# A fixed TensorE order around three places of a hybrid attention block

## The chip, the cores and the metric

The kernel runs on one core of a Trainium2 chip as one program. The metric is device time in microseconds (us) from launch to the end of the program, and smaller is better. The kernel before took 788.79 us (median of three runs, 788.05 to 789.27). Engines are written as in the profile: PE is TensorE's matmuls, PEld its weight loads, DVE is VectorE, ACT is ScalarE, POOL is GpSimd, and SP is the engine whose queue issues most of the transfers.

## The reference, cut to what matters

One block works on 512 tokens of width 1024 in float32. The normed input is projected to the inputs of two mixers. The first is a gated linear attention (GLA) with 4 heads, run forward and backward in chunks. The second is a latent attention (MLA) with 8 heads, whose queries and keys come from normed latents `cq` and `ckv`. Both are gated and added, projected by `w_out` and added to the input. Then follow a norm, an MLP and a last norm:

```python
y_gla = gla_branch(gq, gk, gv, gr, z_gf, z_gb, ...)
y_mla = mla_branch(cq, ckv, kr, positions, ...)
merged = jax.nn.sigmoid(z_ma) * y_gla + jax.nn.sigmoid(z_mb) * y_mla
h = h + merged @ w_out[l]
m = rmsnorm(h, g_mlp[l])
h = h + jnp.square(jax.nn.relu(m @ w_ff1[l])) @ w_ff2[l]
return rmsnorm(h, g_final)
```

In `mla_branch` the query latent is normed before its projection: `q = (rmsnorm(cq, g_q) @ w_uq)`. In `gla_direction` the decayed queries and keys of a chunk give `scores`, which are masked and then multiplied by `v`.

## The kernel before

Every large product is done as three matmuls in the fp32r form (`mm3`, L90): each factor is split into a high half, which ACT writes (`split`, L95, and `split_scaled`, L99: lines L96 and L100), and a rest, which DVE writes (L97, L101). Transposes, GLA scores and feature sums are plain f32 matmuls, which PE runs in two passes. Tokens lie in four row tiles of 128, `h0` to `h3` in the profile's `h`.

Tiles come from pools with a fixed number of buffers. The PSUM pool has two tags, `mm` and `at`, of four banks each. A new tile of a tag takes the bank of the fourth tile before it, so its first matmul waits until that tile has been read for the last time. Weight halves (`wh`, `wl`) have four buffers each, and raw weights (`wf`) three.

The program is written in Python and ordered by a scheduler, which estimates when instructions can start and writes one fixed sequence per engine. On the chip each engine takes its own sequence strictly in that order. An instruction that waits for a semaphore holds everything behind it on its engine. `in_program_order` (L103) can pin a stretch of the program to the order in which it is written, on all engines.

Four places matter here.

**GLA scores** (`gla_scores`, L460). For head h, `bd` gets the four backward diagonal blocks (L463). ACT copies it to `bds`. Then each of four row tiles `sc` gets three matmuls (L475, L476, L477). The second and third read `qk` tiles that POOL scales last (L432). DVE writes the masked backward part into `sc` (`copy_predicated`, L481), and ACT and DVE split `sc` into halves for the output product `gla_out` (L538, tiles `gla..o`). In the main loop the scores of a head come before the gate projection `zb` of feature `2h` (`mla_g2`), which is followed by the gates of the next head (`gatef`, `gateb`, L379) and `zb` of feature `2h+1`. For head 2 the values `gv` are projected just before the scores.

**Query latent** (head 3, `latent`, L568). The sums of squares of `cq` (tile `cqss`) go through DVE and POOL to a diagonal matrix `cqdg` (L257). Two matmuls with ones spread it to `cqrs` (L266). DVE scales the latent (`cqc`, L586), it is split into `cqhl`, and the rotary projections `ro` read it.

**MLP transposes** (`rows_product`, L831, `normed`, L871, and `Flipped`). The second column half of `w_out` ends row by row (tiles `wo`, banks of tag `at`): when a row tile is complete, DVE adds it to `h` (L859), ACT sums squares (L156), DVE and POOL make the row factor (`hp`, L163 and L166), and DVE writes the normed row `ms` (L876). PE then transposes the row in eight pieces into `mb` (L181), and after two rows ACT and DVE split `mb` into the `mT` halves (L100, L101). The first two hidden tiles of the MLP, `f00` and `f01`, run on token halves, so that they can start when rows 0 and 1 are there. DMA loads of the next weights (`f02f` and so on, and 16 pieces `w` of `w_ff2`) stand in SP's queue between.

**The last group.** The second MLP product runs in seven Strassen-like products per group. `prep` makes the halves of the weights for the product after next. In the last group `last_rows` (L1018) pins its order: the last rows are added, squared and scaled (`out_square`, `out_store`), row 1 in two column halves `ge` and `gend`, and the output goes out in eight transfers.

Of the kernel before, what the change touches and what calls it, by code (L numbers as in the profile page):

```python
# [15 lines left out]
ALU = mybir.AluOpType  # L16
AX = mybir.AxisListType

P = 128
S = 512  # L20
NT = S // P
D = 1024
KD = D // P
# [36 lines left out]
def tile_block(ctx: ExitStack, tc: tile.TileContext, t, out: bass.AP):  # L60
    nc = tc.nc
# [38 lines left out]
        nc.scalar.activation(hi, src, AF.Copy, scale=scale)  # L100
        nc.vector.scalar_tensor_tensor(lo, src, scale, raw(hi), op0=ALU.mult, op1=ALU.subtract)  # L101

    def in_program_order(start):  # L103

        prev = {}
        for ins in nc.cur_bb.bb.instructions[start:]:
            before = prev.get(ins.engine)
            if before is not None:
                tc.add_manual_dep(
                    ins, before,  # L110
                    mybir.DependencyInfo(mybir.DependencyClass.NoSync, mybir.DependencyReason.DATA),
                    reason="program order",
                )
            prev[ins.engine] = ins.name


    ident = one([P, P], F32, "ident")
# [96 lines left out]
        wh, wl = weights(w[:, col : col + P], name)  # L214
        return wh, wl, ps(tag, name)

    def proj_run(begun, src, half=None):
        wh, wl, acc = begun
        c = slice(0, S) if half is None else slice(half * 256, half * 256 + 256)
        for k in range(KD):  # L220
            mm3(acc[:, c], wh[:, k, :], wl[:, k, :], src[k][:, 0, c], src[k][:, 1, c], k == 0, k == KD - 1)
        return acc

# [61 lines left out]
    def v_evict(acc, hl, i):  # L285
        split_scaled(hl[:, 0, :], hl[:, 1, :], acc, r_x[:, i : i + 1])

    fixed = len(nc.cur_bb.bb.instructions)
    warm = ps("at", "warm")
    for _ in range(8):  # L290
        nc.tensor.matmul(warm[:, :P], ident, ident, start=True, stop=True)
# [20 lines left out]
    for k in range(KD):  # L312
        wh, wl = (vh[k // 2][x][:, k % 2, :] for x in range(2))
# [220 lines left out]
    def mla_g2(f):  # L534

        return gated(proj_T(C_ZB + f * P, f"zb{f}"), f"b{f}")[1]
# [124 lines left out]
    merged = [None] * MH  # L661
# [98 lines left out]
    y1, g2 = [], []  # L760
# [5 lines left out]
    for h in range(GH):  # L766
        last = h == GH - 1
        if h:
            g1 = gla_g1(h, (0,))
            waiting = gla_rstd(*waiting)  # L770
            g1 += gla_g1(h, (1,))
            y1 += gla_norm(*waiting)
        if h == GH - 2:
            cos, sin = rotary_tables()
        near, nxt, far = gla_qk(h, parts)
        if last:
            ckv_steps, cq_steps = latent(C_CKV, 2, V_KV, "ckv"), latent(C_CQ, 3, V_Q, "cq")
            next(ckv_steps)
            next(ckv_steps)
            next(cq_steps)  # L780
            ckv = next(ckv_steps)
            next(cq_steps)
        if h == 2:
            v = gla_v(1)
        if last:
            cq = next(cq_steps)
        sc = gla_scores(near, nxt, far)
        g2.append(mla_g2(2 * h))
        if last:
            kbuf = rotary_k()  # L790
            ro = rotary_q()
        else:
            parts = gate_parts(h + 1)
        g2.append(mla_g2(2 * h + 1))
        if last:
            for _ in up_units(0):
                pass
        waiting = gla_out(h, sc, v, g1, f"gla{h}"), g1, f"gla{h}"
# [24 lines left out]
    hrow = []  # L823
# [4 lines left out]

    hparts = {}

    def rows_product(lhs, w, nk, name, first_done, done):  # L831
        for c in range(2):
            accs = [ps(("mm", "at")[c], f"{name}{c}{i}") for i in range(NT)]

            def piece(i, k2, wh, wl):
                tok = slice(i * P, (i + 1) * P)
                for kk in range(2):
                    k = 2 * k2 + kk
                    mm3(accs[i], lhs[k][:, 0, tok], lhs[k][:, 1, tok], wh[:, kk, :], wl[:, kk, :],
                        k == 0, k == nk - 1)  # L840

            staggered = 2 if c == 1 else 0
            kept = []
            for k2 in range(nk // 2):
                wh, wl = weights(w[k2 * 2 * P : (k2 + 1) * 2 * P, c * S : (c + 1) * S], f"{name}{c}{k2}")
                if k2 >= nk // 2 - staggered:
                    kept.append((k2, wh, wl))
                    continue
                for i in range(NT):
                    piece(i, k2, wh, wl)  # L850
            for i in range(NT):
                for k2, wh, wl in kept:
                    piece(i, k2, wh, wl)
                add_rows(i, c, accs[i])
                (first_done, done)[c](i)

    def add_rows(i, c, acc):
        hc = hrow[i][:, c * S : (c + 1) * S]
# [12 lines left out]
    def normed(i):  # L871
        m = ms_rows[i]
        square_half(hrow[i], 1, hparts[i], m)
        rs = row_rstd(hparts[i])
        for c in range(2):
            nc.vector.tensor_scalar(  # L876
                m[:, c * S : (c + 1) * S], hrow[i][:, c * S : (c + 1) * S], rs, None, op0=ALU.mult
            )
        fm.rows(i, m)
        if i % 2 == 1:  # L880
            fm.evacuate(i // 2)

    rows_product(merged, t["w_out"][0], KD, "wo", first_half_square, normed)

# [130 lines left out]

    def last_rows(left, right4, right2, x_accs):  # L1018

        begun = len(nc.cur_bb.bb.instructions)  # L1020
        for rb in range(2):
            block_product(4, left, right4, x_accs, False, rb)
            add_rows(2 + rb, 0, x_accs[rb])
            out_square(2 + rb, slice(0, S))
        e_accs = [ps("mm", f"ge{rb}") for rb in range(2)]
        parts = e_accs[1], ps("at", "gend")
        block_product(2, left, right2, e_accs, True, 0)
        out_store(2)
        add_rows(0, 0, e_accs[0])
        out_square(0, slice(0, S))  # L1030
        out_store(3)
        for x in range(2):
            cols = slice(x * HT, (x + 1) * HT)
            block_product(2, left, right2, [None, parts[x]], True, 1, cols, slice(0, HT))
            nc.vector.tensor_tensor(hrow[1][:, cols], parts[x][:, 0:HT], hrow[1][:, cols], op=ALU.add)
            out_square(1, cols, x == 1)
            out_store(x)
        in_program_order(begun)

    early = [proj_begin(w1, j * P, f"f0{j}", "at") for j in range(2)]  # L1040
    for half in range(2):
        for begun in early:
            proj_run(begun, mT, half)
    for x in (B11, B12, B22, B21):
        load_w2(0, x)
    for qd in range(NQ):
# [12 lines left out]
        xs_ = [ps("at", f"gx{qd}{rb}") for rb in range(2)]  # L1059
        zs_ = [ps("at", f"gz{qd}{rb}") for rb in range(2)]  # L1060
        for n, m in enumerate(ORDER):
            if n + 2 < len(ORDER):
                right[ORDER[n + 2]] = prep(ORDER[n + 2], qd)
            if m == 2:
                accs, begin = [ps("mm", f"gw{qd}{rb}") for rb in range(2)], True
            elif m == 4 and last:
# [4 lines left out]
            for rb in range(2):  # L1071
                block_product(m, left, right[m], accs, begin, rb)
                upper, lower = rb, 2 + rb
                if m in (1, 2):
                    add_rows(upper, 0, accs[rb])
                elif m in (6, 3):
                    add_rows(upper, 1, accs[rb])
                elif m in (5, 7):
                    add_rows(lower, 1, accs[rb])
                if m == 4:  # L1080
                    add_rows(lower, 0, accs[rb])
                if last and m in (3, 7):
                    out_first(upper if m == 3 else lower)


def build(arrays):
# [21 lines left out]
```

## Time and profile before

| | |
|---|---|
| Median of three runs | 788.79 us (788.05 to 789.27) |
| Profiled execution: its time | 788.01 us |
| Profiled execution: its span, first to last instruction | 786.3 us |
| PE busy | 773.6 us (98%) |
| PE weight loads busy | 647.6 us (82%) |
| DVE busy | 546.4 us (69%) |
| ACT busy | 409.4 us (52%) |
| POOL busy | 104.4 us (13%) |
| Granted TensorE clock, mean | 0.998 |

The profiled execution took 0.78 us less than the median, and 1.7 us of it lie outside the span. Rows of a timeline read: start in us from the span's start, duration in us, engine, source line, operation, output<-inputs, shapes, count, and in brackets the idle time of the engine just before and what ended it. Neighbouring matmuls overlap in these rows, so their spacing is read from their starts. Line numbers are those of the kernel before.

### The profile page before, as it was taken

Reading aid. Unit: us, or ns where it says so; the run is one execution under the profiler, and the core shown is the slowest. Engines: PE = TensorE matmul, PEld = TensorE weight load, DVE = VectorE, ACT = ScalarE, POOL = GpSimd, SP = SyncE. Lnnn points to the kernel's source line nnn. Section 1 sums busy time; section 2 is a strip of 40 time slices with the busy share of each in tenths; the row PEclk is TensorE's granted clock in tenths of the full one; section 3 lists DMA queues with packets and bytes.
Section 4 is the critical chain, followed back from the end, with each engine's and each line's share of the span. In section 5 each row is a group of like instructions: output and inputs, shape, how many; then the busy total and the mean of one; then the engine's idle time right before and its main releaser. Section 6 shows DMA issues by size and latency. Waiting matters only on the chain.

```text
span 786.3 us, 10004 instructions
## 1 busy us (share of the span) xinstructions
PE 773.6 (98%) x3736; PEld 647.6 (82%) x3736; DVE 546.4 (69%) x839; ACT 409.4 (52%) x685; POOL 104.4 (13%) x168
## 2 busy tenths in 40 slices
PE   9999999999999999999999999999999999999995
PEld 7888888888888878888888888888888888888884
DVE  7767657575565449799973677875787578848785
ACT  8463624523562326698853466535554465336644
POOL 1023203213031214211120100000000000000023
PEclk9999999999999999999999999999999999999999
DMA  7633232233223422513032731164106510560002
GB/s 256 169 85 81 55 90 72 79 94 108 73 62 81 74 46 52 131 55 108 28 135 85 267 105 54 54 185 136 51 15 202 142 48 27 173 176 0 28 1 107
DMA packets 102385, 74.47 MB, mean 95 GB/s; under 512 B 14976, under 2 KB 86656, under 8 KB 102336
## 3 DMA queue, kind: packets, MB, share of 16 engines
q1 hardware_dynamic: 101248, 70.66, 31.5%
q10 hardware_dynamic: 864, 2.38, 0.8%
q0 software_dynamic: 224, 0.79, 0.3%
q8 instruction: 29, 0.48, 0.2%
q14 instruction: 20, 0.16, 0.1%
HBM read 69.62 MB, written 2.10 MB: 91 GB/s over the span
## 4 chain that ended last, share of the span: by engine, by line
PE 92%; issue 3%; DVE 2%; POOL 1%; ACT 1%; POOLq 0%; DVEq 0%
PE f L92 7%; PE f L93 7%; PE f L91 7%; PE gx L91 4%; PE gx L93 4%; PE gx L92 4%; PE gv L301 3%; PE gr L91 2%; PE gr L93 2%; PE gr L92 2%; PE za L93 2%; PE gz L93 2%; PE gz L92 2%; PE gz L91 2%; PE za L92 2%
## 5 line engine op out<-in xcount | busy, mean ns | idle before, releaser
L904 DVE TENSOR_TENSOR w<-w,w 128x1024 f32<-128x1024 f32 x32 | 38.8, 1222 | 0.4
L1058 POOL DMA_DIRECT2D gfin<-in_g_final x1 | 0.7, 653 | 282.7 <-PE f L93 282.7
L725 ACT ACTIVATE e<-s,top 128x512 f32<-128x512 f32 x32 | 21.9, 685 | 6.0 <-DVE top L722 5.1
L97 DVE TENSOR_TENSOR pT<-tp,pT 128x512 fp32r<-128x512 f32 x32 | 21.7, 680 | 0.5 <-ACT pT L96 0.4
L859 DVE TENSOR_TENSOR h<-gx,h 128x512 f32<-128x512 f32 x32 | 21.6, 685 | 0.5 <-PE gx L93 0.4
L722 DVE TENSOR_REDUCE top<-s 128x1 f32<-128x512 f32 x32 | 21.7, 680 | 0.1
L96 ACT ACTIVATE pT<-tp 128x512 fp32r<-128x512 f32 x32 | 18.9, 592 | 3.1 <-PE tp L739 2.9
L739 PE MATMUL tp<-ident,e 128*128 128x128 f32 x128 | 19.2, 273 | 0.1
L91 PE MATMUL av<-pT,v 128*128 128x256 f32 x64 | 19.3, 301 | 0.0
L757 POOL TENSOR_TENSOR tb<-tb,g 128x512 f32<-128x512 f32 x8 | 11.1, 1382 | 56.9 <-DVE tb L756 43.8
L739 PEld LDWEIGHTS tp<-ident,e 128*128 128x128 f32 x128 | 15.3, 140 | 3.9 <-DVE pT L97 0.5
L952 ACT ACTIVATE fa<-f 128x512 f32<-128x512 f32 x32 | 18.5, 577 | 0.0
L92 PE MATMUL av<-pT,v 128*128 128x256 f32 x64 | 18.4, 288 | 0.0
L516 DVE TENSOR_TENSOR za<-za,R 128x512 f32<-128x512 f32 x8 | 5.5, 691 | 18.4 <-PE za L93 18.4
L93 PE MATMUL av<-pT,v 128*128 128x256 f32 x64 | 18.1, 283 | 0.0
L96 ACT ACTIVATE gbh<-y 128x512 fp32r<-128x512 f32 x16 | 10.1, 633 | 14.0 <-DVE y L969 14.0
L432 POOL TENSOR_TENSOR qk<-qkf,e3f 128x256 f32<-128x256 f32 x8 | 7.8, 972 | 63.8 <-DVE qkf L424 63.8
L96 ACT ACTIVATE sc<-sc 128x512 fp32r<-128x512 f32 x16 | 8.8, 599 | 10.6 <-DVE sc L481 10.6
L96 ACT ACTIVATE b_00h<-w 128x1024 fp32r<-128x1024 f32 x7 | 7.4, 1060 | 12.9 <-PE gz L93 6.0
L91 PE MATMUL s<-kbuf,q 128*128 128x512 f32 x32 | 13.7, 428 | 0.3 <-DVE pT L97 0.3
L961 ACT ACTIVATE px<-fa 128x256 f32<-128x256 f32 x32 | 13.4, 419 | 1.0
L96 ACT ACTIVATE b_10h<-w 128x1024 fp32r<-128x1024 f32 x7 | 7.4, 1060 | 12.1 <-PE gz L93 6.0
(1460 smaller groups left out, 2805.6 us busy)
## 6 DMA issues: line engine op xcount, KB each, us to landing
w<-in_w_ff SPq DMA_DIRECT2D x64, 256.0 KB, 3.6
x<-in_xt SPq DMA_DIRECT2D x8, 256.0 KB, 5.2
vw<-in_w_in SPq DMA_DIRECT2D x8, 256.0 KB, 5.3
q<-ro SPq DMA_DIRECT2D x16, 128.0 KB, 4.9
h<-in_x ACTq DMA_DIRECT2D x4, 512.0 KB, 4.7
out<-ms SPq DMA_DIRECT2D x7, 256.0 KB, 2.3
gr0f<-in_w_in SPq DMA_DIRECT2D x1, 512.0 KB, 4.8
za0f<-in_w_in SPq DMA_DIRECT2D x1, 512.0 KB, 5.7
```

The costliest lines, as they stand in the source:

```text
L91: nc.tensor.matmul(acc, lh, rh, start=start, stop=False, skip_group_check=onto)
L92: nc.tensor.matmul(acc, lh, rl, start=False, stop=False, skip_group_check=onto)
L93: nc.tensor.matmul(acc, ll, rh, start=False, stop=stop, skip_group_check=onto)
L96: nc.scalar.activation(hi, src, AF.Copy)
L97: rest.tensor_tensor(lo, src, raw(hi), op=ALU.subtract)
L301: nc.tensor.matmul(v_accs[i], a[:, i * P : (i + 1) * P], b, start=k == 0 and x == 0, stop=k == KD - 1 and x == 2)
L722: nc.vector.tensor_reduce(top, acc, axis=AX.X, op=ALU.max, negate=True)
L725: nc.scalar.activation(e, acc, AF.Exp, bias=top, accum_out=tot)
L739: nc.tensor.transpose(tp[:, k * P : (k + 1) * P], e[:, k * P : (k + 1) * P], ident)
L859: nc.vector.tensor_tensor(hc, acc, hc, op=ALU.add)
L904: nc.vector.tensor_tensor(wq[dst][g], wq[x][g], wq[y][g], op=op)
L952: nc.scalar.activation(a, acc, AF.Relu)
```

## The change

Four edits; no arithmetic is added or taken away.

1. For heads 0, 1 and 3 the gate projection `zb` of feature `2h` is written ahead of the scores, and a helper `tensor_engine_goes_on` makes PE's first scores matmul come after the last matmul of that projection. Head 2 keeps its order.
2. For head 3 the spreading of the query latent's factor is written behind the scores, and PE is made to take it after them.
3. In `rows_product` the last two k-steps of the second column half are regrouped. Rows 0 and 1 are completed first. Row 2 runs its first half, then come the transposes of row 0, then its second half; row 3 likewise around the transposes of row 1. The transposes of rows 2 and 3 move behind five of the eight k-steps of `f01` on the first token half. `f00` and `f01` alternate by k on the second half. PE is pinned to this order from the start of the regrouped part to the end of `f01`; the other engines are left to the scheduler.
4. In the last group, `prep` for product 2 is written behind the additions of product 7 (before, ahead of the product). In `last_rows`, row 1's two column halves are now added one behind the other, then squared one behind the other, and then rows 0 and 1 are stored.

```diff
--- before.py
+++ after.py
@@ -100,18 +100,34 @@
         nc.scalar.activation(hi, src, AF.Copy, scale=scale)
         nc.vector.scalar_tensor_tensor(lo, src, scale, raw(hi), op0=ALU.mult, op1=ALU.subtract)
 
-    def in_program_order(start):
+    def issued_after(ins, before):
+        tc.add_manual_dep(
+            ins, before,
+            mybir.DependencyInfo(mybir.DependencyClass.NoSync, mybir.DependencyReason.DATA),
+            reason="program order",
+        )
+
+    def traced():
+        return len(nc.cur_bb.bb.instructions)
+
+    def in_program_order(start, engines=None):
 
         prev = {}
         for ins in nc.cur_bb.bb.instructions[start:]:
+            if engines is not None and ins.engine not in engines:
+                continue
             before = prev.get(ins.engine)
             if before is not None:
-                tc.add_manual_dep(
-                    ins, before,
-                    mybir.DependencyInfo(mybir.DependencyClass.NoSync, mybir.DependencyReason.DATA),
-                    reason="program order",
-                )
+                issued_after(ins, before)
             prev[ins.engine] = ins.name
+
+    PE_ONLY = (mybir.EngineType.PE,)
+
+    def tensor_engine_goes_on(start, mid):
+
+        ins = nc.cur_bb.bb.instructions
+        pe = [[i for i in part if i.engine in PE_ONLY] for part in (ins[start:mid], ins[mid:])]
+        issued_after(pe[1][0], pe[0][-1].name)
 
 
     ident = one([P, P], F32, "ident")
@@ -214,10 +230,10 @@
         wh, wl = weights(w[:, col : col + P], name)
         return wh, wl, ps(tag, name)
 
-    def proj_run(begun, src, half=None):
+    def proj_run(begun, src, half=None, ks=range(KD)):
         wh, wl, acc = begun
         c = slice(0, S) if half is None else slice(half * 256, half * 256 + 256)
-        for k in range(KD):
+        for k in ks:
             mm3(acc[:, c], wh[:, k, :], wl[:, k, :], src[k][:, 0, c], src[k][:, 1, c], k == 0, k == KD - 1)
         return acc
 
@@ -285,7 +301,7 @@
     def v_evict(acc, hl, i):
         split_scaled(hl[:, 0, :], hl[:, 1, :], acc, r_x[:, i : i + 1])
 
-    fixed = len(nc.cur_bb.bb.instructions)
+    fixed = traced()
     warm = ps("at", "warm")
     for _ in range(8):
         nc.tensor.matmul(warm[:, :P], ident, ident, start=True, stop=True)
@@ -782,11 +798,19 @@
             next(cq_steps)
         if h == 2:
             v = gla_v(1)
+        begun = traced()
+        if h == 2:
+            sc = gla_scores(near, nxt, far)
+            g2.append(mla_g2(2 * h))
+        else:
+            g2.append(mla_g2(2 * h))
+            gated_at = traced()
+            sc = gla_scores(near, nxt, far)
+            tensor_engine_goes_on(begun, gated_at)
         if last:
+            scored_at = traced()
             cq = next(cq_steps)
-        sc = gla_scores(near, nxt, far)
-        g2.append(mla_g2(2 * h))
-        if last:
+            tensor_engine_goes_on(gated_at, scored_at)
             kbuf = rotary_k()
             ro = rotary_q()
         else:
@@ -828,7 +852,7 @@
 
     hparts = {}
 
-    def rows_product(lhs, w, nk, name, first_done, done):
+    def rows_product(lhs, w, nk, name, first_done, done, flip):
         for c in range(2):
             accs = [ps(("mm", "at")[c], f"{name}{c}{i}") for i in range(NT)]
 
@@ -848,11 +872,33 @@
                     continue
                 for i in range(NT):
                     piece(i, k2, wh, wl)
-            for i in range(NT):
-                for k2, wh, wl in kept:
-                    piece(i, k2, wh, wl)
+            if c == 0:
+                for i in range(NT):
+                    add_rows(i, c, accs[i])
+                    first_done(i)
+                continue
+            begun = traced()
+            ks = [(2 * k2 + kk, wh[:, kk, :], wl[:, kk, :]) for k2, wh, wl in kept for kk in range(2)]
+
+            def part(i, which):
+                tok = slice(i * P, (i + 1) * P)
+                for k, wh, wl in ks[which]:
+                    mm3(accs[i], lhs[k][:, 0, tok], lhs[k][:, 1, tok], wh, wl, k == 0, k == nk - 1)
+
+            def complete(i):
                 add_rows(i, c, accs[i])
-                (first_done, done)[c](i)
+                done(i)
+
+            whole, first, rest = slice(0, 4), slice(0, 2), slice(2, 4)
+            for i in range(2):
+                part(i, whole)
+                complete(i)
+            for i in range(2):
+                part(2 + i, first)
+                flip(i)
+                part(2 + i, rest)
+                complete(2 + i)
+            return begun
 
     def add_rows(i, c, acc):
         hc = hrow[i][:, c * S : (c + 1) * S]
@@ -876,11 +922,13 @@
             nc.vector.tensor_scalar(
                 m[:, c * S : (c + 1) * S], hrow[i][:, c * S : (c + 1) * S], rs, None, op0=ALU.mult
             )
-        fm.rows(i, m)
+
+    def flipped(i):
+        fm.rows(i, ms_rows[i])
         if i % 2 == 1:
             fm.evacuate(i // 2)
 
-    rows_product(merged, t["w_out"][0], KD, "wo", first_half_square, normed)
+    begun = rows_product(merged, t["w_out"][0], KD, "wo", first_half_square, normed, flipped)
 
 
 
@@ -1017,7 +1065,7 @@
 
     def last_rows(left, right4, right2, x_accs):
 
-        begun = len(nc.cur_bb.bb.instructions)
+        begun = traced()
         for rb in range(2):
             block_product(4, left, right4, x_accs, False, rb)
             add_rows(2 + rb, 0, x_accs[rb])
@@ -1029,18 +1077,26 @@
         add_rows(0, 0, e_accs[0])
         out_square(0, slice(0, S))
         out_store(3)
+        cols = [slice(x * HT, (x + 1) * HT) for x in range(2)]
         for x in range(2):
-            cols = slice(x * HT, (x + 1) * HT)
-            block_product(2, left, right2, [None, parts[x]], True, 1, cols, slice(0, HT))
-            nc.vector.tensor_tensor(hrow[1][:, cols], parts[x][:, 0:HT], hrow[1][:, cols], op=ALU.add)
-            out_square(1, cols, x == 1)
+            block_product(2, left, right2, [None, parts[x]], True, 1, cols[x], slice(0, HT))
+            nc.vector.tensor_tensor(hrow[1][:, cols[x]], parts[x][:, 0:HT], hrow[1][:, cols[x]], op=ALU.add)
+        for x in range(2):
+            out_square(1, cols[x], x == 1)
+        for x in range(2):
             out_store(x)
         in_program_order(begun)
 
     early = [proj_begin(w1, j * P, f"f0{j}", "at") for j in range(2)]
-    for half in range(2):
-        for begun in early:
-            proj_run(begun, mT, half)
+    proj_run(early[0], mT, 0)
+    proj_run(early[1], mT, 0, range(5))
+    flipped(2)
+    flipped(3)
+    proj_run(early[1], mT, 0, range(5, KD))
+    for k in range(KD):
+        for e in early:
+            proj_run(e, mT, 1, (k,))
+    in_program_order(begun, PE_ONLY)
     for x in (B11, B12, B22, B21):
         load_w2(0, x)
     for qd in range(NQ):
@@ -1059,8 +1115,10 @@
         xs_ = [ps("at", f"gx{qd}{rb}") for rb in range(2)]
         zs_ = [ps("at", f"gz{qd}{rb}") for rb in range(2)]
         for n, m in enumerate(ORDER):
-            if n + 2 < len(ORDER):
-                right[ORDER[n + 2]] = prep(ORDER[n + 2], qd)
+            ahead = ORDER[n + 2] if n + 2 < len(ORDER) else None
+            behind = last and ahead == 2
+            if ahead and not behind:
+                right[ahead] = prep(ahead, qd)
             if m == 2:
                 accs, begin = [ps("mm", f"gw{qd}{rb}") for rb in range(2)], True
             elif m == 4 and last:
@@ -1081,6 +1139,8 @@
                     add_rows(lower, 0, accs[rb])
                 if last and m in (3, 7):
                     out_first(upper if m == 3 else lower)
+            if behind:
+                right[ahead] = prep(ahead, qd)
 
 
 def build(arrays):
```

## The prediction

> **What bounds the kernel now.** I read the page first: the span and the chain that ended last.
>
> ```profile
> span 786.3 us, 10004 instructions
> PE 92%; issue 3%; DVE 2%; POOL 1%; ACT 1%; POOLq 0%; DVEq 0%
> ```
>
> PE is the bound nearly everywhere, and no edit takes a matmul away. So the change can win only where PE stands still, or behind its last matmul. The waits of PE come next; columns are the sum in us, the count and the longest. The two rows behind them are pieces of the chain that ended last, in order of time.
>
> ```profile
> PE cqrs L266 <- DVE cqdg L257: 1.1, 2, 0.6
> PE mb L181 <- DVE ms L876: 0.9, 2, 0.5
> PE sc L477 <- POOL qk L432: 0.8, 2, 0.4
> PE gx L91 <- DVE h L859: 0.3, 1, 0.3
> ```
>
> ```profile
> 1.52 3.64 PE warm L291 x16
> 5.17 16.62 PE gv L301 x72
> ```
>
> The four edits aim at these four waits, 3.1 us in all, and at the tail. A 512-wide matmul takes 16.62 / 72 = 0.23 us from start to start, half that when 256 wide. Starts of matmuls show each wait a little longer than its row, since overlap is lost too. So each place is costed from starts, and from what every engine's new sequence puts ahead of the awaited instruction. Those sequences come from comparing the order of instructions in the two built programs; all durations below are from the trace of before.
>
> **Edit 1, scores of heads 0 and 1.** First the scores block of head 0, then that of head 2, which never waits.
>
> ```profile
> 69.31 1.16 PE L463 MATMUL bd<-qkb 128*128 128x128 f32 x8
> 74.31 0.58 PE L92 MATMUL zb<-xT,zb0h 128*128 128x512 f32 x1
> ...
> 200.97 1.05 PE L463 MATMUL bd<-qkb 128*128 128x128 f32 x8
> 204.50 0.38 PE L475 MATMUL sc<-qkf 128*128 128x128 f32 x2
> 205.19 0.58 PE L91 MATMUL zb<-xT,zb4h 128*128 128x512 f32 x1
> ...
> 77.72 1.06 ACT L96 ACTIVATE gr3h<-gr3f 128x1024 fp32r<-128x1024 f32 x1 [0.80 <-PE zb L92]
> 78.82 1.22 DVE L97 TENSOR_TENSOR gr3l<-gr3f,gr3h 128x1024 fp32r<-128x1024 f32 x1 [0.22 <-ACT gr3h L96]
> ```
>
> From `bd` to the next product: 74.31 - 69.31 = 5.00 us against 205.19 - 200.97 = 4.22, so the wait costs 0.78, twice over the two heads: 1.56. With all of `zb` ahead, `bd` starts 14 matmuls (3.2 us) later, at 72.5, and POOL's tiles are there.
>
> The same 14 matmuls were the cover of what follows: `gatef` and `gateb` take the PSUM banks of the first two `sc` tiles and wait for their split. Now the splits stand behind `zb`'s work. ACT starts `gr3h` at 72.5 (1.06), then the gate and `bds` (0.6 each, by the gate's row in edit 2), until 74.6; DVE has `gr3l` (1.22) from 73.6 to 74.8, then two masked copies and two rests (0.2 and 0.6 each, rows in edit 2). The first split ends near 76.5, the second near 77.2; PE wants the banks at 76.9 and 77.1. So up to 0.1 us of wait per head. I take -1.5; ends -1.6 (no wait) and -1.2 (0.2 per head).
>
> **Edit 2, query latent of head 3.** The rows show PE around the two waits, then the DVE and ACT work that the new sequences put ahead.
>
> ```profile
> 291.15 0.39 PE L93 MATMUL zb<-xT,zb6l 128*128 128x512 f32 x1
> 297.67 0.58 PE L91 MATMUL ro<-cqhl,wr0h 128*128 128x512 f32 x1
> ...
> 291.99 1.51 DVE L257 TENSOR_TENSOR cqdg<-ident,cqrl 128x512 fp32r<-128x512 f32 x1
> 297.70 0.90 DVE L481 COPY_PREDICATED sc<-after,bds 128x128 f32<-128x128 int32 x4
> 299.11 2.48 DVE L97 TENSOR_TENSOR sc<-sc,sc 128x512 fp32r<-128x512 f32 x4
> 301.60 0.72 DVE L649 TENSOR_SCALAR krsin<-sin,gvec 64x512 f32<-64x512 f32 x1
> ...
> 299.95 0.65 ACT L518 ACTIVATE tb<-zb 128x512 f32<-128x512 f32 x1
> ```
>
> Before, PE is free at 291.38 and begins `ro` at 297.67; the content is 4.22 for the scores and 0.45 for `cqrs`, so 1.6 us are idle. In the new sequence the wait for `cqdg` goes. But `cqrs` now takes the bank of the first `sc` tile, so it waits for that tile's split; the first `gla3o` product, which stands next, waits for the second. On DVE, `cqdg` ends at 293.5; then come `zb` (like a rest, 0.6, to 294.1), `krsin`, `kswap`, three masked copies and `kr`, and only then the first rest. On ACT the gate `tb` waits for that `zb` and stands ahead of `bds`: 294.1 plus twice 0.6 is 295.3. Two stalls follow. The fourth `sc` tile needs the bank of `bd`: PE would start it at 291.38 + 3.53 = 294.9 and gets it at 295.3 (0.4). Masked copies from 295.3 (0.2 each), `kr` (taken as a rest, 0.6) from 295.9, first rest 296.5 to 297.2: PE, done with the scores at 296.2, waits 1.05. `cqrs` takes 0.45, and the second rest, at 297.85, costs 0.15 more. Together 1.6 us idle, as before: I take 0.0. The ends: -0.3 if the 64-row steps run shorter than their rows, +0.8 if each takes its row's full length, as beside POOL's work. Behind it, `ro`'s halves are ready at each use by my times (the closest, 300.1 for a use at 300.2).
>
> **Edit 3, transposes.** PE's markers, then DVE and POOL (`hp`: least, median and longest in ns), then the `w` transfers with their first reader.
>
> ```profile
> 436.00 0.39 PE L93 MATMUL wo<-wo13h,mg 128*128 128x512 f32 x1
> 447.49 0.28 PE L91 MATMUL f<-mT,f00h 128*128 128x256 f32 x1
> 450.36 0.28 PE L91 MATMUL f<-mT,f01h 128*128 128x256 f32 x1
> 460.91 0.40 PE L91 MATMUL f<-mT,f02h 128*128 128x512 f32 x1
> ...
> 436.43 0.69 DVE L859 TENSOR_TENSOR h<-wo,h 128x512 f32<-128x512 f32 x1 [0.35 <-PE wo L93]
> 438.82 0.88 DVE L876 TENSOR_SCALAR ms<-h,hp 128x512 f32<-128x512 f32 x2 [0.68 <-POOL hp L166]
> 444.89 3.23 DVE L101 SCALAR_TENSOR_TENSOR mT<-mb,gvec,mT 128x256 fp32r<-128x256 f32 x8 [0.97 <-ACT mT L100]
> 449.23 1.22 DVE L97 TENSOR_TENSOR f02l<-f02f,f02h 128x1024 fp32r<-128x1024 f32 x1
> ...
> L166 POOL TENSOR_TENSOR hp<-hp,mhalf x8: 548/561/1182, 438.2 to 781.0; 128x1 f32<-128x1 f32 x8
> ...
> 436.56 10.89 SPq L900 DMA_DIRECT2D w<-in_w_ff  x16
> 466.35 1.06 ACT L96 ACTIVATE b_00h<-w 128x1024 fp32r<-128x1024 f32 x1 [0.82 <-PE f L92]
> w<-in_w_ff SPq DMA_DIRECT2D x64, 256.0 KB, 3.6
> ```
>
> A row needs 439.70 - 436.43 = 3.27 us from its addition to its normed end. Row 0 is normed at 439.7 and now flipped at 440.3, row 1 at 442.9 and 444.0, so both waits at `mb` go, and PE reaches `f00` at 446.3 instead of 447.49: -1.2.
>
> What is late next is `mT`. Row 2 is now complete at 442.6, before the first flips end, and the scheduler puts its whole norm and `f02l` ahead of the eight `mT` rests on DVE: addition 442.85, plus 3.27 is 446.1, plus 1.1 for `f02l` (its row less the overlap of neighbours) is 447.2, against 444.89 before. `f00`'s second matmul needs the first rest, at 447.6, and then goes at the pace of the rests (3.23 / 8 = 0.40 each, against 0.36 for three matmuls of (450.36 - 447.49) / 24 = 0.12). The last is there at 450.4, so `f01` begins at 450.7 instead of 450.36. The 1.2 us are spent, and 0.3 more. Row 3 is added behind the rests (450.3); with another weight rest of 1.1 on its way it is normed at 453.5 and 453.8, and PE, at its transposes at 453.35, waits 0.1. The second half alternates two tiles per k (0.72 us against 0.40 per rest), so it doesn't wait: `f02` begins near 461.3 instead of 460.91. I take +0.4; ends -0.8 (`f02l` not in the way) and +1.0 (POOL's step at its longest, 1.18 instead of 0.56).
>
> In SP's queue `f05f` now stands ahead of the 16 `w` pieces and waits for `f02l`, so they go out from 447.7 to 458.6, 11 us later. Their first reader is a weight split at 466.35, and a piece lands in 3.6 us: the first four are there at 454. Hidden, and the cover is 12 us.
>
> **Edit 4.** In the built programs DVE's sequence around product 2's halves is the same as before (addition of row 2, half, addition of row 3, half). So the 0.3 us wait of `gx` stays: 0. In the tail the sequence does change:
>
> ```profile
> 778.35 0.28 PE L93 MATMUL gend<-b_31h,ga 128*128 128x256 f32 x1
> 781.63 0.75 DVE L1013 SCALAR_TENSOR_TENSOR ms<-h,hp,gfin 128x512 f32<-128x512 f32 x1 [0.66 <-POOL hp L166]
> 777.52 0.99 POOL L166 TENSOR_TENSOR hp<-hp,mhalf 128x1 f32<-128x1 f32 x1 [1.61 <-DVE hp L163]
> 779.86 0.33 SPq L1015 DMA_DIRECT2D out<-ms  x1
> 782.44 0.33 SPq L1015 DMA_DIRECT2D out<-ms  x1
> GB/s 0 0 0 0 0 0 0 233 378 366 397 240 0 0 0 265 384 391 384 189 139 384 391 366 334 0 0 0 202 372 391 384 265 0 0 0 0 0 0 0
> ```
>
> The last row of numbers is the DMA rate from 774 to 787 us in slices of 0.325 us. `gend` is added as soon as it is complete, at 778.7, no longer behind row 0's output step; its square follows the first half's, and POOL's power starts near 780.0. Row 0's output step (0.75) now runs beside it, as one did beside the row of 0.99, so row 1's output runs from 781.05 to 781.8: 0.6 earlier. But row 0's transfers, before issued from 779.86, wait for that step, to 780.67. Then four transfers of 256 KB leave in one burst: 1.05 MB at 390 GB/s is 2.7 us, data begin 0.7 to 0.9 after the issue (782.44 to slice 28, at 783.1 to 783.4), so 781.5 + 2.7 = 784.2 against 784.7 at the end of the last burst before (slice 32). I take -0.4; ends -1.0 and +0.1.
>
> The Trainium skill, "DMA: Bandwidth & Descriptors", section "Specifications", puts the limit of HBM for one core at about 358 GB/s. By it the burst would take 2.9 us, an estimate, and the whole sum would come to -1.3 instead of -1.5. The slices above show 384 to 397, so I stay with the trace.
>
> **The sum.** -1.5 + 0.0 + 0.4 - 0.4 = -1.5 us. The profiled execution took 788.01 (span 786.3 and 1.7 around it), 0.78 under the median of the runs, 788.79. I carry the difference to the median: 787.3.
>
> **The rivals.** (a) The fixed order works as drawn and neither score splits nor `mT` hold PE: 1.56 + 1.6 + 1.2 + 0.4 = 4.8 less, 784.0. For it: each old wait is really moved off. Against it: the sequences of DVE and ACT put other work ahead, and engines don't reorder. (b) The order costs what it gains: the latent's stall at its end of +0.8, the rest as forecast, 788.1. For it: `krsin`'s length without POOL is not in the trace. (c) Slower: the TensorE clock falls in a new stall. In the `warm` row at the start 16 passes took 3.64 us; eight like them take 1.05 in `bd`'s row, 0.12 each when an estimated 0.1 for the end of the last is left out. So one warm-up cost 3.64 - 1.9 = 1.7 us. If each of the two new stalls of 1.05 and 1.2 us brought one, the time would be 787.3 + 3.4 = 790.7, and one alone just brings it above before's. Against it: the clock stayed full over the 0.6 us waits now (0.998 in the mean), and no stall nears the length of the warm-up. The Trainium skill, "TensorE: Matmul & The Clock Gate", Part 1, says an idle window of about 3.4 us is needed; no run here shows where between 0.6 and 3.6 us it lies.
>
> **How the numbers follow.** Within 0.2% is 1.6 us either way, about what a measurement of this kernel can tell from no change. The forecast has 0.66 and lies on that border: 0.36 beyond it, 0.30 within. (a) has 0.14, (b) 0.12, (c) 0.08. So faster 0.50, same 0.42, slower 0.08. The low ends add to -3.7 and the high ends to +0.7, 785.1 to 789.5; I take 785.0 to 789.2, which leaves out (c) and most of (a).
>
> **What would show it.** Right: no wait of `sc` for POOL and none of `mb` for `ms` in heads 0 and 1 and rows 0 and 1; `cqrs` waiting about 1 us, for a rest of `sc`; `f00` taking 4.4 us from its first matmul to `f01`'s instead of 2.9; the last four transfers in one burst. Wrong: `f00` in 2.9 us, or `cqrs` without a wait, or `gateb` waiting over 0.3 us, which would show that the cover by `zb` was needed.

## The result, and the profile after

The changed kernel took 786.52 us in the median (785.83 to 786.97), against 788.10 for the kernel before on the same chips. The ratio is 0.9978, with a 95% interval of 0.9969 to 0.9987: about 1.7 us less, and 0.7 us either way. The forecast was 787.3, which is 1.5 us under the 788.79 it started from. The profiled execution of the changed kernel took 786.52 too. From its page and its waits of PE (sum in us, count, longest):

```profile
span 784.8 us, 10007 instructions
PE 92%; issue 3%; DVE 3%; ACT 1%; POOL 1%; POOLq 0%; DVEq 0%; ACTq 0%
```

```profile
PE cqrs L282 <- DVE sc L97: 1.2, 1, 1.2
PE f L92 <- DVE mT L101: 1.1, 1, 1.1
...
PE sc L491 <- ACT bds L483: 0.2, 1, 0.2
PE gx L91 <- DVE h L905: 0.2, 1, 0.2
```

Three waits of the list before are gone (`sc` for `qk`, `cqrs` for `cqdg`, `mb` for `ms`), and two new ones stand there, at the places that the prediction named, each a little over 1 us (a third, of `sc` for `bds`, is 0.2). Only the first of the three was won for good. This shows when the span is cut at matmuls that both kernels share. Each column is the distance between two starts in the profiled execution, in us; the last column runs from the last matmul's start to the end of the span. The last row is after less before.

| profiled execution | to the last `gv` of the first pair | to `gv` of the second pair (edit 1) | to the first `s` of attention (edit 2) | to the first `wo` | to `f02` (edit 3) | to the last matmul | to the end (edit 4) |
|---|---|---|---|---|---|---|---|
| before | 27.80 | 151.41 | 140.22 | 80.09 | 61.40 | 317.44 | 7.93 |
| changed | 28.09 | 149.99 | 140.41 | 80.11 | 61.47 | 317.28 | 7.48 |
| difference | +0.29 | -1.42 | +0.19 | +0.02 | +0.07 | -0.16 | -0.45 |

The first column depends on when the first loads land; it lay between 27.8 and 28.5 us over all kernels of this study, so parts of a microsecond are read from the other columns and not from totals. Where nothing was changed, those of edits 1 and 3 repeat within 0.05 us and the others within 0.1, all but edit 2's, of which more below.

**Edit 1.** Head 0 of the changed kernel, as a timeline of PE, then of DVE and ACT:

```profile
72.77 1.05 PE L479 MATMUL bd<-qkb 128*128 128x128 f32 x8
...
76.99 0.58 PE L395 MATMUL gatef<-z,gate_f 128*128 128x512 f32 x1
77.42 0.47 PE L395 MATMUL gateb<-z,gate_b 128*128 128x512 f32 x1
...
75.98 1.29 DVE L97 TENSOR_TENSOR sc<-sc,sc 128x512 fp32r<-128x512 f32 x2
```

From `bd` to the next product are 4.22 us, the content alone, as in head 2 before. The first two rests of `sc` end at 77.27, one 0.6 us earlier, so `gatef` and `gateb` find their banks free at 76.99 and 77.42, with 0.3 and 0.15 us to spare. The cover by `zb` was not needed.

**Edit 2.** Head 3, around the latent: PE, then POOL and DVE.

```profile
294.14 0.49 PE L491 MATMUL sc<-qkf 128*128 128x128 f32 x2 [0.23 <-ACT bds L483]
296.50 0.70 PE L282 MATMUL cqrs<-cqdg,ones_r 128*128 128x512 f32 x2 [1.22 <-DVE sc L97]
297.10 0.47 PE L91 MATMUL gla3o<-sc,gv 128*128 128x512 f32 x1
...
290.79 1.00 POOL L97 TENSOR_TENSOR wq0l<-wq0f,wq0h 128x384 fp32r<-128x384 f32 x1 [1.08 <-ACT wq0h L96]
...
290.84 1.50 DVE L273 TENSOR_TENSOR cqdg<-ident,cqrl 128x512 fp32r<-128x512 f32 x1
292.26 0.68 DVE L532 TENSOR_TENSOR zb<-zb,R 128x512 f32<-128x512 f32 x1
292.97 0.49 DVE L665 TENSOR_SCALAR krsin<-sin,gvec 64x512 f32<-64x512 f32 x1
293.49 0.69 DVE L666 TENSOR_TENSOR kswap<-kswap,krsin 64x512 f32<-64x512 f32 x1
294.21 0.70 DVE L497 COPY_PREDICATED sc<-after,bds 128x128 f32<-128x128 int32 x3
294.95 0.69 DVE L668 TENSOR_TENSOR kr<-kr,kswap 64x512 f32<-64x512 f32 x1
295.67 1.89 DVE L97 TENSOR_TENSOR sc<-sc,sc 128x512 fp32r<-128x512 f32 x3
```

DVE goes from `cqdg` to the first rest of `sc` without a pause, exactly in the order that the prediction listed, and `cqrs` starts soon after the first rest's end (295.67 + 1.89 / 3 = 296.30, against 296.50). The two waits are 0.23 and 1.22 us.

**Edit 3.** PE, then DVE:

```profile
445.25 0.28 PE L91 MATMUL f<-mT,f00h 128*128 128x256 f32 x1
446.61 0.39 PE L92 MATMUL f<-mT,f00h 128*128 128x256 f32 x1 [1.08 <-DVE mT L101]
...
449.69 0.28 PE L91 MATMUL f<-mT,f01h 128*128 128x256 f32 x1
...
444.94 1.22 DVE L97 TENSOR_TENSOR f02l<-f02f,f02h 128x1024 fp32r<-128x1024 f32 x1
446.07 3.22 DVE L101 SCALAR_TENSOR_TENSOR mT<-mb,gvec,mT 128x256 fp32r<-128x256 f32 x8
```

`f00` takes 449.69 - 445.25 = 4.44 us to `f01`'s start; before it took 2.87. The rests of `mT` come behind `f02l`.

**Edit 4.** The tail, and the DMA rate from 774 to 787 us in slices of 0.325 us:

```profile
777.34 0.28 PE L93 MATMUL gend<-b_31h,ga 128*128 128x256 f32 x1
...
778.81 0.74 DVE L1061 SCALAR_TENSOR_TENSOR ms<-h,hp,gfin 128x512 f32<-128x512 f32 x1
780.00 0.75 DVE L1061 SCALAR_TENSOR_TENSOR ms<-h,hp,gfin 128x512 f32<-128x512 f32 x1 [0.44 <-POOL hp L182]
...
778.98 0.99 POOL L182 TENSOR_TENSOR hp<-hp,mhalf 128x1 f32<-128x1 f32 x1 [1.48 <-DVE hp L179]
...
779.58 0.33 SPq L1063 DMA_DIRECT2D out<-ms  x1
...
780.78 0.33 SPq L1063 DMA_DIRECT2D out<-ms  x1
GB/s 0 0 0 0 271 384 385 403 170 0 0 0 321 391 359 384 158 0 0 82 372 391 378 384 366 384 397 378 95 0 0 0 0 0 0 0 0 0 0 0
```

The four last stores leave in one burst, eight full slices long, at 366 to 397 GB/s.

### The profile page after: what moved, and what is told of

The parts are those of the page before. It is cut to its first block, busy times and chain, and to the rows that moved or that the text cites. A ratio compares the mean times of both kernels' runs of the same rounds, so it can differ in the third digit from the quotient of the medians.

```text
span 784.8 us, 10007 instructions
## 1 busy us (share of the span) xinstructions
PE 773.0 (98%) x3736; PEld 648.1 (83%) x3736; DVE 546.6 (70%) x839; ACT 409.9 (52%) x685; POOL 103.7 (13%) x168
## 4 chain that ended last, share of the span: by engine, by line
PE 92%; issue 3%; DVE 3%; ACT 1%; POOL 1%; POOLq 0%; DVEq 0%; ACTq 0%
PE f L92 7%; PE f L93 7%; PE f L91 7%; PE gx L91 4%; PE gx L93 4%; PE gx L92 4%; PE gv L317 3%; PE gr L91 2%; PE gr L93 2%; PE gz L91 2%; PE za L93 2%; PE gr L92 2%; PE gz L93 2%; PE za L91 2%; PE gz L92 2%
## 5 line engine op out<-in xcount | busy, mean ns | idle before, releaser
L96 ACT ACTIVATE b_20h<-w 128x1024 fp32r<-128x1024 f32 x7 | 7.4, 1060 | 12.1 <-PE gz L93 6.0
```

What stands on the lines that cost most here:

```text
L96: nc.scalar.activation(hi, src, AF.Copy)
```

## The experiments

Each run is compared with the kernel before on its own chip; ratios carry 95% intervals. Beside them stand the columns of the cut that differ from the changed kernel's.

**Edit 1 alone.** The kernel before, with this in the main loop and the helper from the diff:

```diff
-        sc = gla_scores(near, nxt, far)
-        g2.append(mla_g2(2 * h))
+        begun = traced()
+        if h < 2:
+            g2.append(mla_g2(2 * h))
+            gated_at = traced()
+            sc = gla_scores(near, nxt, far)
+            tensor_engine_goes_on(begun, gated_at)
+        else:
+            ...
```

> The kernel before with edit 1 alone, for heads 0 and 1. Theory (the gain of the change is the two waits of sc for POOL's qk, 0.78 us each): 1.5 us less than the kernel before, no wait of sc for qk, and no wait over 0.1 us of gatef or gateb in their place. Rival (zb was needed as cover for the splits, and the gain came from the other edits): the wait comes back at gatef or gateb and the time is within 0.5 us of the kernel before.

786.62 us, ratio 0.9982 (0.9974 to 0.9991). The column of edit 1 is 149.97. Its waits of PE:

```profile
PE cqrs L282 <- DVE cqdg L273: 1.1, 2, 0.6
PE mb L197 <- DVE ms L899: 0.8, 2, 0.5
...
PE gx L91 <- DVE h L882: 0.2, 1, 0.2
```

The waits for `qk` are gone, nothing stands in their place, and the other old waits are all still there. Edit 1 alone gives what the whole change gives, as far as the intervals can tell. Two more things are seen here: the stretch from `f02` to the last matmul is 317.27 us without edit 4, so its 0.16 us less are not that edit's, and neither is `gx`'s shorter wait. What makes them was not tried.

**Edit 2 undone.** In the changed kernel the factor is spread ahead of the scores again, and head 3 has its old order:

```diff
+        if last:
+            cq = next(cq_steps)
         begun = traced()
-        if h == 2:
+        if h >= 2:
             sc = gla_scores(near, nxt, far)
...
         if last:
-            scored_at = traced()
-            cq = next(cq_steps)
-            tensor_engine_goes_on(gated_at, scored_at)
```

> The changed kernel with edit 2 alone undone: the factor of the query latent is spread ahead of the scores again, zb6 and the scores in their old order. Theory (the edit exchanged one stall of about 1.6 us for another of about 1.5): the waits of cqrs for cqdg return, 1.1 us, the waits of cqrs and sc for DVE and ACT go, and the time stays within 0.4 us of the changed kernel. Rival (the new stall is the whole cost of edit 2, and the old wait was hidden): 1.2 us less than the changed kernel.

786.12 us, ratio 0.9974 (0.9964 to 0.9983); the column of edit 2 is 140.11 instead of 140.41. The old wait did not come back whole: `cqrs` waits 0.6 us once, and `s` waits 0.5 us for a transfer instead:

```profile
PE cqrs L282 <- DVE cqdg L273: 0.6, 1, 0.6
PE s L91 <- DMA q<-ro: 0.5, 1, 0.5
```

By this pair edit 2 costs 0.3 us; the next run shows why the pair is not quite a fair one.

**Edit 3 undone.** `rows_product` and the early products `f00` and `f01` as before, in the changed kernel.

> The changed kernel with edit 3 alone undone. Theory (two mb waits of 0.9 us in all against one wait of f00 for mT of 1.1 us): within 0.4 us of the changed kernel, the mb waits back, f00's first token half 2.9 us long again instead of 4.4. Rival (the regrouping saves the mb waits and the wait of f00 would be there anyway): 0.9 to 1.2 us more than the changed kernel, with the wait of f00 for mT in the trace beside the mb waits.

786.33 us, ratio 0.9975 (0.9964 to 0.9985). The column of edit 3 is 61.40 against 61.47, with the two `mb` waits (0.8) back and `f00`'s gone: one stall was exchanged for another of its size. But the column of edit 2 is also 0.64 us shorter here, 139.77, though nothing was touched there. The rows:

```profile
290.65 0.69 DVE L273 TENSOR_TENSOR cqdg<-ident,cqrl 128x512 fp32r<-128x512 f32 x1
...
290.63 1.56 POOL L97 TENSOR_TENSOR wq0l<-wq0f,wq0h 128x384 fp32r<-128x384 f32 x1 [1.10 <-ACT wq0h L96]
```

The same two instructions as above, and on PE, DVE, ACT and POOL everything up to them comes in the same order as in the changed kernel, but here the long one is POOL's. The run with edit 2 undone was of this kind too (0.68 us for `cqdg`). Compared within a kind, edit 2 costs 0.2 us where POOL is first (140.41 against 140.19 with edit 1 alone) and saves 0.3 where DVE is first (139.77 against 140.11). In the old order the kind hardly matters (140.19 against 140.11); there `s` waits for the transfer when `cqrs` comes earlier. Each number is one profiled execution.

**Edit 4 undone.** The last group as before, in the changed kernel.

> The changed kernel with edit 4 alone undone. Theory (the earlier addition of row 1's second half saves 0.5 us behind the last matmul, and the moved prep 0.15 us ahead of it): the stretch from the last matmul's start to the end of the span is 7.95 us again instead of 7.46, the wait of gx for h 0.3 instead of 0.2, the time 0.65 us more than the changed kernel. Rival (the four stores leave in one burst, so the end doesn't move): the stretch within 0.15 us of 7.46.

787.03 us, ratio 0.9983 (0.9974 to 0.9992). From the last matmul's start to the end are 785.33 - 777.40 = 7.93 us again, against 7.48: the reordered tail is worth 0.45 us. The part of the expectation on `gx` failed: its wait stays at 0.2 and the stretch ahead at 317.32. Moving `prep` for product 2 does nothing, as the prediction had it.

**The side work behind the latent.** In head 3 of the changed kernel, the gate of `zb6` and the rotary key go behind the latent's steps on DVE, and their ACT work behind `bds` (`scaled_ins` and `bds_ins` are noted in lines not shown):

```diff
...
+            side = traced()
+            g2.append(gated(acc, f"b{2 * h}")[1])
             kbuf = rotary_k()
+            for i in nc.cur_bb.bb.instructions[side:]:
+                if i.engine == mybir.EngineType.DVE:
+                    issued_after(i, scaled_ins.name)
+                elif i.engine == mybir.EngineType.Activation:
+                    issued_after(i, bds_ins.name)
```

> The changed kernel with DVE's and ACT's work on the gate of zb6 and on the rotary key (krsin, kswap, kr) taken behind the latent's own steps in head 3. Theory (cqrs waits because this work stands ahead of the first rest of sc): no wait of cqrs, none of sc for bds, 1.4 us less than the changed kernel (785.1). Rival (the rests themselves, or cqdg's end at 292.3, hold cqrs): the wait of cqrs stays above 0.6 us, or comes back as a wait of ro, and the time stays within 0.5 us of the changed kernel.

788.44 us, ratio 1.0006 (0.9997 to 1.0015): all of the gain is gone. `cqrs` waits no more, as the theory had it, but `gla3o` waits 0.4 us for a rest of `sc`, and the column of edit 2 is 142.62, 2.2 us longer. (DVE was ahead of POOL here, `cqdg` 0.69 us; against the 139.77 of the like case it is 2.85.) Its waits of PE, and busy times in two stretches (span, PE, PEld, DVE, ACT, POOL):

```profile
PE uv L91 <- DVE rob L655: 1.6, 1, 1.6
...
PE gla3rs L282 <- ACT e L741: 0.6, 1, 0.6
PE s L91 <- DMA q<-ro: 0.5, 1, 0.5
PE gla3o L91 <- DVE sc L97: 0.4, 1, 0.4
```

```profile
304.00:310.00 6.00, 6.00 (x28) 4.98 (x27) 5.88 (x8) 4.11 (x9) 3.29 (x5) 1.00 0.42 98
310.00:316.00 6.00, 4.39 (x31) 3.82 (x30) 5.87 (x8) 3.22 (x8) 4.25 (x5) 1.00 0.18 30
```

DVE is busy 5.88 and 5.87 of 6 us. The work that was pushed back runs into the rotation of `ro`, whose last reader `rob` starts at 312.20 us (308.16 in the changed kernel), so `uv` waits for a PSUM bank. The expectation stopped at `ro` and did not follow DVE's queue past it. The side work stood in a better place before: what follows needs DVE more than the scores do.

**Another bank for the factor.** One line, in the changed kernel:

```diff
-        rs = ps("at", f"{name}rs")
+        rs = ps("mm" if name == "cq" else "at", f"{name}rs")
```

> The changed kernel with cqrs in a bank of the other PSUM tag, so that it need not wait for the first sc tile's split. Theory (the first rest of sc is late, whoever waits for it): cqrs goes without a wait, gla3o then waits some 0.6 to 0.9 us for the same rest, since it reads it, and 0.3 to 0.6 us are saved. Rival (the bank alone is the cause): no wait in either place, 1.2 us less than the changed kernel.

785.54 us, ratio 0.9965 (0.9952 to 0.9978); the column of edit 2 is 139.13. PE:

```profile
294.24 0.81 PE L282 MATMUL cqrs<-cqdg,ones_r 128*128 128x512 f32 x2
295.55 0.50 PE L91 MATMUL gla3o<-sc,gv 128*128 128x512 f32 x1 [0.50 <-DVE sc L97]
```

`cqrs` runs without a wait, and `gla3o` waits 0.50 us for the same rest. DVE was ahead of POOL here, as with edit 3 undone, whose column is 139.77; so of the 1.28 us that the column is shorter, 139.77 - 139.13 = 0.64 us are the bank's. So the bank was about half of `cqrs`'s wait, and the late rest holds `gla3o` for the other half.

**POOL's weight rest later.** ACT's `wq0h`, which releases POOL's `wq0l`, pinned behind the latent's last split `cq_end` (noted in a line not shown):

```diff
...
+        at = traced()
         split(wqh, wql, wq, nc.gpsimd)
+        if pr == 0:
+            issued_after(nc.cur_bb.bb.instructions[at], cq_end)
```

> The changed kernel with ACT's wq0h, and so POOL's rest wq0l, behind the latent's last split. In the changed kernel wq0l begins on POOL 0.05 us ahead of the second half of cqdg on DVE, which then takes 1.50 us instead of 0.69. Theory (DVE stands still while POOL's tensor operation runs): cqdg's second half takes 0.69, the first rest of sc is 0.8 us earlier, the wait of cqrs 0.4 to 0.6 instead of 1.2, sc's wait for bds is gone, 0.6 to 0.8 us less in all. Rival (cqdg is long for another reason, its operands or the order on DVE): it stays at 1.5 and the time is the changed kernel's.

786.57 us, ratio 0.9978 (0.9969 to 0.9987). With `wq0l` away, `cqdg`'s second half takes 0.69 us and the column is 139.79, as with edit 3 undone. But the next column is 0.60 longer (80.71 against 80.11), with a new wait of 0.4 us at `gla3ss` for DVE. The mechanism holds, the total doesn't move. How POOL's later work leads to the new wait was not traced: `gla3sq`, which `gla3ss` waits for, took 0.91 us on DVE there, against 0.68 in the changed kernel. `cqrs` still waits 1.0 us, not 0.4 to 0.6, since PE arrives earlier without `sc`'s wait.

**The weights behind row 3's norm.** In the changed kernel, the splits of `f02` and `f03` on ACT and DVE come behind the norm of row 3 (`norm_end`, noted in lines not shown), so behind the first eight `mT` rests:

```diff
...
+            if qd == 0 and j < 4:
+                for ins in nc.cur_bb.bb.instructions[start:]:
+                    if ins.engine in (mybir.EngineType.Activation, mybir.EngineType.DVE):
+                        issued_after(ins, norm_end[ins.engine])
```

> The changed kernel with the splits of the weights f02 and f03 (ACT and DVE) pinned behind row 3's norm, so that the eight mT rests follow row 2's norm at once. Theory (f02l ahead of the rests holds f00): f00's wait for mT 0.1 instead of 1.1 us, then f00 still paced by the rests (0.38 per k), f02 of the second half's end 1.1 us earlier, 1.1 us less than the changed kernel. Rival (row 2's norm, not f02l, holds the rests, or row 3 comes late and mb waits): under 0.5 us less, with the wait still at f00 or a new one at mb for ms.

786.12 us, ratio 0.9974 (0.9964 to 0.9983); the column of edit 3 is 61.12. The first half's wait is gone, but `f00`'s second half now has one, since both weights stand ahead of that half's rests. PE, then DVE:

```profile
454.46 0.39 PE L92 MATMUL f<-mT,f00h 128*128 128x256 f32 x1 [0.53 <-DVE mT L101]
...
452.79 1.22 DVE L97 TENSOR_TENSOR f03l<-f03f,f03h 128x1024 fp32r<-128x1024 f32 x1
453.93 2.44 DVE L101 SCALAR_TENSOR_TENSOR mT<-mb,gvec,mT 128x256 fp32r<-128x256 f32 x6
```

**One weight in each gap.** `f02` as there, `f03` behind the second half's rests (`flip_end`, noted likewise); against the run above:

```diff
             if qd == 0 and j < 4:
+                ends = norm_end if j == 2 else flip_end
...
-                        issued_after(ins, norm_end[ins.engine])
+                        issued_after(ins, ends[ins.engine])
```

> The changed kernel with f02's splits behind row 3's norm, as in the run with both weights pinned, but f03's behind the second half's mT rests. Theory (each token half of f00 waits for what DVE and ACT put ahead of that half's rests): no wait of f00 in either half over 0.1 us, f02 begins 1.0 us earlier, 1.0 us less than the changed kernel (785.5). Rival (DVE is full here, so that the time comes back in front of f02 or f03): the wait moves to f for f03's or f04's split and the gain is under 0.4 us.

784.68 us, ratio 0.9966 (0.9954 to 0.9977). The column of edit 3 is 60.34, 1.13 us shorter, and no wait of `f` is left. With `f02l` out of the way, edit 3 gives the 1.1 us that its two `mb` waits cost.

**Row 0's output between.** In `last_rows` of the changed kernel:

```diff
-        for x in range(2):
-            out_square(1, cols[x], x == 1)
-        for x in range(2):
-            out_store(x)
+        out_square(1, cols[0], False)
+        p = hparts[1]
+        nc.scalar.activation(ms_rows[1][:, cols[1]], hrow[1][:, cols[1]], AF.Square, accum_out=p[:, 1:2])
+        out_store(0)
+        row_rstd(p)
+        out_store(1)
```

> The changed kernel with row 0's output step on DVE directly behind the additions, ahead of row 1's last factor, so that POOL's power runs while DVE stands still. Theory (the end hangs on row 1's chain and on the one burst of four stores): row 0's stores leave 0.6 us earlier, POOL's power takes 0.55 instead of 0.99, row 1's output runs 0.3 us earlier, and the stretch from the last matmul's start to the end of the span is 7.1 us instead of 7.46. Rival (the DMA's own landing time sets the end): row 1's output is earlier but the stretch stays within 0.1 us of 7.46.

785.42 us, ratio 0.9971 (0.9960 to 0.9983). DVE, POOL and SP's queue:

```profile
779.03 0.75 DVE L1061 SCALAR_TENSOR_TENSOR ms<-h,hp,gfin 128x512 f32<-128x512 f32 x1 [0.67 <-POOL hp L182]
...
778.44 0.55 POOL L182 TENSOR_TENSOR hp<-hp,mhalf 128x1 f32<-128x1 f32 x1 [1.48 <-DVE hp L179]
...
778.32 0.33 SPq L1063 DMA_DIRECT2D out<-ms  x1
...
779.81 0.33 SPq L1063 DMA_DIRECT2D out<-ms  x1
```

The last matmul starts at 776.80 and the span ends at 783.66: 6.86 us, against 7.48. POOL's power takes 0.55 us with DVE standing still, 0.99 beside DVE's output step. (The column of edit 2 was the short one here, 139.73: DVE was ahead of POOL, as with edit 3 undone.)

**Together.** The own bank, one weight in each gap and row 0's output between, in one kernel.

> The changed kernel with cqrs in the other tag's bank, f02's and f03's splits pinned as in the run that splits them up, and row 0's output between. If the three gains add (0.6 without the chance position of POOL's wq0l, 1.0 and 0.3 us): 784.6, 3.5 us less than the kernel before. If DVE gives one of them back elsewhere: 785.5 or more.

783.36 us, ratio 0.9948 (0.9935 to 0.9960): 4.1 us less than the kernel before by the ratio, and the fastest of the study. The columns are 139.07, 60.34 and 6.83, together 1.34 + 1.13 + 0.65 = 3.12 us shorter than the changed kernel's, so the gains add. Expected were 1.9; of the rest, some 0.64 us are DVE ahead of POOL in this execution, and 0.35 the tail. By the medians the three add 2.4 us to the change's 1.7, with intervals of 0.7 and 1.0 us either way.

## Why the prediction was right

The sign, the size and the mechanisms came out as forecast. The time of 787.3 lies 0.8 us above the measured one, since the 788.79 it started from, a median of three runs, lies 0.7 above the median of eleven. By its steps, in us:

- **Edit 1, -1.5:** measured -1.42, and alone -1.44. The 0.1 us per head for the splits did not appear as a wait.
- **Edit 2, 0.0:** measured +0.19. The two new stalls were there, 0.23 and 1.22 us in the list of waits. Counted from starts, as the forecast counts, they are larger: the fourth `sc` tile could have begun at 290.22 + 3.53 = 293.75 and began at 294.14, 0.39 for a forecast 0.4; PE would then be done with the scores 0.9 later, at 295.04, and `cqrs` began at 296.50, 1.46 for a forecast 1.05. So the second stall is the term that was too small: DVE's first rest came 295.67 - 290.84 = 4.83 after `cqdg`'s second half began, priced at 296.5 - 291.99 = 4.51. Half of the 0.4 was made good further on; at which step was not followed. What the price also hid is that `cqdg`'s row of 1.51 us, taken over as it stood, was itself DVE and POOL colliding. In seven of the twelve other profiled kernels it took 0.69, and the column was then 0.6 us shorter where head 3 had the changed kernel's order. The price holds where POOL goes first, as in both executions compared.
- **Edit 3, +0.4:** measured +0.07. `f00` to `f01` took 4.44 us, forecast 4.4, and the cause was `f02l`, as the runs with it moved show. PE reached `f00` 1.32 earlier, counted from the first `wo`, for a forecast 1.2. Mis-sized is mainly what follows: row 3's transposes were forecast to wait 0.1 us and did not, and from `f01` to `f02` the changed kernel needs 460.06 - 449.69 = 10.37 us against 10.55 before. The forecast carried 10.6 over.
- **Edit 4, -0.4:** measured -0.45 for the tail, and nothing for `prep`. POOL's power took 0.99 us beside DVE's step, as forecast.
- **Rival (b)**, the latent's stall at +0.8: not so, `krsin` took 0.49 us and the 64-row steps 0.69.
- **Rival (a)**, all stalls vanish: wrong as drawn, since two of the three stalls came back behind DVE's other work. The combined kernel, with the splits of `f02` and `f03` moved, `cqrs` in another bank and a new tail, comes to 4.1 less than before of the 4.8 it drew.
- **Rival (c)**, a slower clock: did not come true. In the two new stalls the granted clock (the 1.00 in these rows of the changed kernel) stays full:

```profile
295.00:297.00 2.00, 0.78 (x4) 0.30 (x2) 1.97 (x4) 1.12 (x3) 0.00 (x0) 1.00 0.00 0
446.00:447.00 1.00, 0.39 (x3) 0.40 (x4) 1.00 (x4) 1.00 (x3) 0.00 (x0) 1.00 0.00 0
```

The Trainium skill, "TensorE: Matmul & The Clock Gate", Part 1, has the clock fall only after an idle window of about 3.4 us. Waits of 1.2 us without a fall agree with it, as does the wait of 1.6 us at `uv` in the run with the side work behind, in whose row from 310 to 316 us the granted clock is 1.00; no run here shows what a longer one would do.

The steps add to -1.42 + 0.19 + 0.07 - 0.45 = -1.61, the forecast to -1.5. That they agree so well is partly luck: edits 2 and 3 were off by +0.2 and -0.3, which cancel.

## What to carry to other kernels

A fixed order on the busiest engine only wins where the awaited work is really done earlier. Where the other engines are left to a scheduler, moving PE's wait lets them put other work in front of what PE waits for next, and the stall comes back a little further on; list each engine's new sequence ahead of the awaited instruction before a gain is booked. Give each piece of side work its own gap: moved in a block it closed one stall and opened another, twice in this study.

## What the hardware showed

`cqdg`'s second half on DVE (two operands in SBUF) and POOL's `wq0l` become ready at nearly the same time in head 3, and one of them always takes longer: it ends 0.55 us (DVE) or 0.86 us (POOL) after the other, not far short of its whole length of 0.69 or 1.00. Among the twelve profiled kernels in which both run there, DVE's recorded start follows POOL's by 10 to 23 ns in six, and then DVE takes 0.68 to 0.69 us and POOL 1.55 to 1.57; it follows by 25 to 44 ns in the other six, and then DVE takes 1.50 to 1.52 and POOL 1.00 to 1.01. So a difference of a few ns goes with who pays, and in the changed kernel's order PE's column moves by 0.6 us with it, although the instructions are the same. The Trainium skill, "SBUF — State Buffer", section "Who interferes with whom", says that a DVE instruction with two SBUF inputs contends with a GpSimd instruction that reads SBUF, and that the order of issue decides who blocks. The rows agree that one of the two loses; that the recorded start of POOL's instruction can lie 23 ns ahead and still lose is seen only here.

A kernel's profiled execution can therefore sit 0.6 us off another's although no edit touched the place, which is a third of what this change is worth. Whether the outcome belongs to the kernel or changes from one execution to the next is not shown: each kernel has one profile.
